# A network in one launch: the norms' sums of squares behind a stage's first tile, their broadcast behind the second

## The chip, the cores and the metric

The kernel runs on one core of one Trainium2 chip. The metric is the time of one execution in microseconds of device time; medians of several runs are compared. The profile is of one further execution, and its times count from the first instruction of that execution to the last (the span).

## The reference

Two models follow one another on a sequence of 256 tokens of width 1024, in fp32. The first has a Mamba-2 mixer, a convolutional feed-forward block, a differential attention and a second feed-forward block; the second has a block with a sparse attention and a recurrent unit, whose normalised input is scaled and shifted by a conditioning vector, then a feed-forward block and a last norm. Each of these parts begins with the same step:

```
def rms_norm(x, g):
    xf = x.astype(jnp.float32)
    y = xf * lax.rsqrt(jnp.mean(xf * xf, axis=-1, keepdims=True) + EPS)
    return y.astype(x.dtype) * g

zxbcdt = rms_norm(x, ln_g) @ in_w                                # mamba
u = causal_dwconv(rms_norm(x, ln_g) @ up_w, conv_w, conv_b)      # ffn
kv = rms_norm(x, kv_ln_g) @ kv_w                                 # attn
xn = rms_norm_2(h, g_mix[l]) * (1.0 + sc1) + sh1                 # dsa
return rms_norm_2(h, g_final)
```

So a norm over the 1024 features of a token stands in front of every large product, and it needs all of x.

## The kernel before

The activations lie with the features on the partitions: x is 8 tiles (k = 0 to 7) of 128 features x 256 tokens. Every weight is streamed from memory (tile raw, by the queue of SP) and split into a high half wh (ScalarE, L253) and a low half wl (VectorE, L257, or in certain places GpSimd, L255, chosen by the table POOLED). The operand x is split alike, into xh and xl. An output tile of 128 rows is 8 k with three matmuls each, xh with wh, xl with wh and xh with wl (L379 to L381), 24 matmuls that accumulate in a PSUM tile mm.

A stage (mamba, ffn0, attn, ffn1, dsa, ffn2, final, in this order) starts as follows. As the stage before ends, add_x makes x tile by tile (L509 or L511), square has ScalarE square each (L440) and GpSimd add the squares of k = 1 to 6 to those of k = 0 in sqacc (L444); the square of k = 7 stays apart. mkraw makes for each k the raw operand rw, g times x without the norm, its high half on ScalarE (L396) and its low half on VectorE (L397). The first four tiles of a stage (NRAW; in mamba one narrow tile of 32 rows, for dt, stands ahead of them) are raw tiles: tileR multiplies the weights with rw, and its postponed part f multiplies the result with the norm afterwards (ru, L412, VectorE, reading PSUM). In dsa and ffn2 f also adds a column, rc (ScalarE, L415). In attn the tokens are the rows of the output, so the norm is a scale of rows and no broadcast is needed.

The norm itself is in rstd_bc: the sums over features are matmuls of squares with ones (L452), sqacc first and the last square behind it, each for two halves of the tokens. rsqrt works out the reciprocal root on VectorE (L296) and GpSimd (L297, to the power of -1/2). Then bcast (L463) spreads it over the partitions by two matmuls with the identity, and ScalarE copies it out as rsb (L484). From rsb VectorE makes for each k the normalised ny (L493), ScalarE xh (L468 or L497) and VectorE xl (L469 or L498), which the tiles from the fifth on read. In mamba and the ffn stages (the table DEFER, which holds how many k go with a step) all this, sums included, is issued at once after the first raw tile (self.pre in tileR); in dsa and attn the sums are issued ahead of the first tile.

What is written in this order isn't what runs: a scheduler puts every engine's instructions in an order of its own, by dependencies and by its costs; after(a, b) tells it that a comes behind b on the same engine. later(n, fn) postpones fn by n tiles. There are three mm tiles in PSUM, and five slots each for wh and wl.

## Time and profile before

| | us |
|---|---|
| median of 3 runs | 1180.02 |
| lowest and highest run | 1178.07, 1181.65 |
| the profiled execution | 1182.38 |
| its span | 1180.6 |

In the profiled execution TensorE is busy for 1124.2 us, VectorE for 961.2, ScalarE for 712.3 and GpSimd for 221.3; the mean granted clock of TensorE is 0.977 of full speed. The page gives the busy time of each engine and the costliest groups; a table lists what TensorE waited for; the timelines give each instruction with its start and length, and in brackets the idle time ahead of it and what ended that. A matmul's length there includes its way through the array, and matmuls overlap, so the cost of one in a row of them is the distance between starts. Each fp32 sum or broadcast matmul of the program shows as two in the trace.

### The profile page before, as it was taken

The numbers are of one execution on the slowest core, as the hardware profiler recorded it, in microseconds if no ns is written. First come the engines' busy times: TensorE is split into PE (matmuls) and PEld (weight loads), VectorE is DVE, ScalarE is ACT, GpSimd is POOL, SyncE is SP. The second block draws the span as 40 slices with busy tenths as digits, with TensorE's granted clock in tenths as the row PEclk, the third lists the DMA queues.
The fourth block names the chain that finished last, engine by engine and source line by source line (L and its number), as shares of the span: only waits on it lengthen the run. The fifth ranks groups of instructions, "written<-read, shape, count | busy, mean of one in ns | idle before, by whom it ended". The sixth has DMA issues, their size and how long they took to land.

```text
span 1180.6 us, 23536 instructions
## 1 busy us (share of the span) xinstructions
PE 1124.2 (95%) x9174; PEld 1093.4 (93%) x9174; DVE 961.2 (81%) x1866; ACT 712.3 (60%) x1322; POOL 221.3 (19%) x180
## 2 busy tenths in 40 slices
PE   6899898999999999999899999899999998999997
PEld 5799887989999999988899999899999998999997
DVE  5887998789898878787899998768967888888752
ACT  6567655566666546877466664465587656666541
POOL 3202665242100114222320001100100023200010
PEclk8899989999999999999799999999999999999999
DMA  8455442647756886663456668754452653554530
GB/s 304 140 179 193 152 161 72 219 166 252 266 201 223 275 288 221 190 224 131 168 198 206 207 215 286 250 194 149 170 170 88 223 197 124 205 189 175 172 137 36
DMA packets 50190, 224.80 MB, mean 190 GB/s; under 512 B 5744, under 2 KB 10496, under 8 KB 31136
## 3 DMA queue, kind: packets, MB, share of 16 engines
q1 hardware_dynamic: 41616, 211.53, 52.1%
q10 hardware_dynamic: 7056, 7.46, 2.1%
q0 software_dynamic: 1408, 4.32, 1.2%
q8 instruction: 72, 1.18, 0.4%
q14 instruction: 38, 0.31, 0.1%
HBM read 222.11 MB, written 4.25 MB: 192 GB/s over the span
## 4 chain that ended last, share of the span: by engine, by line
PE 51%; DVE 17%; issue 7%; DMA 7%; ACT 4%; POOL 1%; ACTq 0%; POOLq 0%; DVEq 0%
PE mm L379 15%; PE mm L380 14%; PE mm L381 14%; DMA ada<-in_wada_dram 7%; DVE wl L257 4%; DVE ada L553 2%; DVE cv L818 2%; ACT wh L253 1%; DVE ny L493 1%; PE mm L790 1%; DVE M L705 1%; PE mm L791 1%; PE mm L789 1%; PE mm L921 1%; PE mm L922 1%
## 5 line engine op out<-in xcount | busy, mean ns | idle before, releaser
L253 ACT ACTIVATE wh<-raw 128x1024 fp32r<-128x1024 f32 (+2 forms) x360 | 369.7, 1030 | 264.9 <-PE mm L380 230.4
L257 DVE TENSOR_TENSOR wl<-raw,wh 128x1024 fp32r<-128x1024 f32 (+1 forms) x333 | 397.9, 1195 | 99.5 <-ACT wh L253 96.7
L379 PE MATMUL mm<-xh,wh 128*128 128x256 f32 x1624 | 465.3, 287 | 8.8 <-DVE cv L818 3.4
L380 PE MATMUL mm<-xl,wh 128*128 128x256 f32 x1624 | 460.6, 284 | 6.3 <-DVE xl L469 6.3
L381 PE MATMUL mm<-xh,wl 128*128 128x256 f32 x1624 | 459.8, 283 | 0.0
L379 PEld LDWEIGHTS mm<-xh,wh 128*128 128x128 f32 x1624 | 308.0, 190 | 15.8 <-issue 6.8
L380 PEld LDWEIGHTS mm<-xl,wh 128*128 128x128 f32 x1624 | 308.0, 190 | 8.2 <-DVE xl L469 7.8
L381 PEld LDWEIGHTS mm<-xh,wl 128*128 128x128 f32 x1624 | 308.0, 190 | 0.3 <-DVE xc L1219 0.3
L444 POOL TENSOR_TENSOR sqacc<-sqacc,sq 128x256 f32<-128x256 f32 x42 | 49.6, 1180 | 558.9 <-ACT sq L440 557.3
L379 PE MATMUL mm<-hh,wh 128*128 128x256 f32 x528 | 147.7, 280 | 0.0
L380 PE MATMUL mm<-hl,wh 128*128 128x256 f32 x528 | 147.5, 279 | 0.0
L381 PE MATMUL mm<-hh,wl 128*128 128x256 f32 x528 | 147.2, 279 | 0.0
L818 DVE SCALAR_TENSOR_TENSOR cv<-mm,par,cv 128x255 f32<-128x255 f32 x240 | 114.2, 477 | 4.4 <-ACT cv L816 2.8
L380 PEld LDWEIGHTS mm<-hl,wh 128*128 128x128 f32 x528 | 99.2, 188 | 0.0
L381 PEld LDWEIGHTS mm<-hh,wl 128*128 128x128 f32 x528 | 99.2, 188 | 0.0
L379 PEld LDWEIGHTS mm<-hh,wh 128*128 128x128 f32 x528 | 99.2, 188 | 0.0
L255 POOL TENSOR_TENSOR wl<-raw,wh 128x1024 fp32r<-128x1024 f32 x27 | 71.9, 2662 | 131.5 <-ACT wh L253 126.3
L553 DVE SCALAR_TENSOR_TENSOR ada<-ada,silu_c 128x512 f32<-128x512 f32 x96 | 71.2, 744 | 20.9 <-DMA ada<-in_wada_dram 20.9
L816 ACT ACTIVATE cv<-mm,par 128x256 f32<-128x256 f32 x120 | 65.6, 547 | 0.0
L379 PE MATMUL mm<-rw,wh 128*128 128x256 f32 (+2 forms) x168 | 51.5, 308 | 10.0 <-ACT wh L253 8.9
L380 PE MATMUL mm<-rw,wh 128*128 128x256 f32 (+2 forms) x168 | 52.5, 312 | 0.0
L381 PE MATMUL mm<-rw,wl 128*128 128x256 f32 (+2 forms) x168 | 51.5, 306 | 0.0
(305 smaller groups left out, 1925.4 us busy)
## 6 DMA issues: line engine op xcount, KB each, us to landing
raw<-in_w_dram SPq DMA_DIRECT2D x148, 1024.0 KB, 4.9
ada<-in_wada_dram SPq DMA_DIRECT2D x96, 256.0 KB, 3.7
raw<-in_w_dram SPq DMA_DIRECT2D x23, 896.0 KB, 4.6
raw<-in_w_dram SPq DMA_DIRECT2D x6, 768.0 KB, 4.4
abc<-acs_scr ACTq DMA_DIRECT2D x16, 256.0 KB, 3.3
rel_bias_scr<-rel_bias_row POOLq DMA_DIRECT2D x8, 384.0 KB, 7.0
bias<-rel_bias_scr ACTq DMA_DIRECT2D x16, 128.0 KB, 2.7
x<-in_xT_dram SPq DMA_DIRECT2D x4, 256.0 KB, 4.5
```

Of the source, the lines that this page charges most:

```text
L253: nc.scalar.activation(wh[:, :n], src, AF.Copy)
L255: nc.gpsimd.tensor_tensor(wl[:, :n], src, wh[:, :n].bitcast(F32), op=ALU.subtract)
L257: self.pace = nc.vector.tensor_tensor(wl[:, :n], src, wh[:, :n].bitcast(F32), op=ALU.subtract)
L379: nc.tensor.matmul(out, h, xh[:, k, :], start=first and a == 0, stop=False)
L380: nc.tensor.matmul(out, h, xl[:, k, :], start=False, stop=False)
L381: nc.tensor.matmul(out, l, xh[:, k, :], start=False, stop=last and a == n - 1)
L444: nc.gpsimd.tensor_tensor(self.acc, self.acc, s, op=ALU.add)
L493: nc.vector.scalar_tensor_tensor(y, self.x[:, k, :], g(k), self.rsb, op0=ALU.mult, op1=ALU.mult)
L553: i = nc.vector.scalar_tensor_tensor(t, t, 1.0, self.sc[:, h * 512:h * 512 + 512], op0=ALU.mult, op1=ALU.mult, accum_out=self.part[:, h, m ...
L705: nc.vector.tensor_tensor(mv[:, h, 0:3:2], e[:, h, 0:3:2, :], CB[:, t // 4, 0:3:2, :], op=ALU.mult)
L816: nc.scalar.activation(c, pt, AF.Identity, scale=w(2), bias=P(cb, ct))
L818: nc.vector.scalar_tensor_tensor(c[:, d:], pt[:, :T - d], w(2 - d), c[:, d:], op0=ALU.mult, op1=ALU.add)
```

## The change

mmB keeps its last matmul. What norm leaves for tileR is now a list of two parts: the sums, which are put behind the last matmul of the first raw tile (by after), and the start (broadcast, rsb and all that follows), put behind the last matmul of the second. The multiplication by the norm of the first raw tile is postponed by one tile more. The square of k = 6 stays apart too, so GpSimd adds those of k = 1 to 5 only, and TensorE sums sqacc and two squares, with six matmul instructions instead of four. dsa gets the same treatment as the ffn stages (DEFER), and in attn the sums stand behind the first half tile (tok). In mamba the load of the silu table, and with it what was flushed there, moves into post_dt.

```diff
-DEFER = {"mamba": 2, "ffn": 8}
+DEFER = {"mamba": 2, "ffn": 8, "dsa": 8}
...
-            nc.tensor.matmul(out, l, xh[:, k, :], start=False, stop=last and a == n - 1)
+            self.last_mm = nc.tensor.matmul(out, l, xh[:, k, :], start=False, stop=last and a == n - 1)
...
+        lag = 1
         if self.pre:
-            self.pre()
-            self.pre = None
+            self.pre.pop(0)(self.last_mm)
+            lag = 2 if len(self.pre) else 1
...
-        self.later(1, f)
+        self.later(lag, f)
...
-        if k == 7:
+        if k == 6:
+            self.sq6 = s
+        elif k == 7:
             self.sq7 = s
...
-    def bcast(self, rs):
+    def bcast(self, rs, behind=None):
...
+            if behind is not None:
+                self.after(mm, behind)
...
-        def start():
-            bc = self.rstd_bc([self.acc, self.sq7], D)
+        def sums(behind=None):
+            self.rstd_bc([self.acc, self.sq6, self.sq7], D, bcast=False, behind=behind)
+
+        def start(behind=None):
+            bc = self.bcast(self.rs, behind)
...
         if self.part_of in DEFER:
-            self.pre = start
+            self.pre = [sums, start]
         else:
+            sums()
             start()
...
+            self.table("silu_and_others")
 
         self.tileR("ssm_in_w", rw, False, post_dt, m=32)
-        self.flush()
-        self.table("silu_and_others")
...
-        self.rstd_bc([self.acc, self.sq7], D, bcast=False)
-        rs = self.rs
...
+                if not norm:
+                    self.rstd_bc([self.acc, self.sq6, self.sq7], D, bcast=False, behind=mm)
+                    norm.append(self.rs)
...
-        self.rstd_bc([self.acc, self.sq7], D, bcast=False)
+        self.rstd_bc([self.acc, self.sq6, self.sq7], D, bcast=False)
```

TensorE at the start of mamba, before: the last matmul of the narrow dt tile (32 rows), the sums (ax from onec and a square), four matmuls of the next raw tile, and the broadcast (ax from con and rs).

```order
L381 MATMUL mm<-rw,wl 32x256
L452 MATMUL ax<-onec,sqacc 128x1 x2
L452 MATMUL ax<-onec,sq 128x1 x2
L379 MATMUL mm<-rw,wh 128x256
L380 MATMUL mm<-rw,wh 128x256
L381 MATMUL mm<-rw,wl 128x256
L379 MATMUL mm<-rw,wh 128x256
L463 MATMUL ax<-con,rs 128x128 x2
```

The same place now, the sums first (the lines of the changed kernel are numbered one to a dozen higher):

```order
L382 MATMUL mm<-rw,wl 32x256
L457 MATMUL ax<-onec,sqacc 128x1 x2
L457 MATMUL ax<-onec,sq 128x1 x4
L380 MATMUL mm<-rw,wh 128x256
L381 MATMUL mm<-rw,wh 128x256
```

And TensorE 24 matmuls further on, where that raw tile ends:

```order
L382 MATMUL mm<-rw,wl 128x256
L470 MATMUL ax<-con,rs 128x128 x2
L380 MATMUL mm<-rw,wh 128x256
L381 MATMUL mm<-rw,wh 128x256
L382 MATMUL mm<-rw,wl 128x256
```

The sums kept their place, with two instructions more, and the broadcast moved from 4 to 24 matmuls behind them.

TensorE at the start of dsa, before, where the sums of sqacc stand ahead of the first raw tile and those of the last square behind 16 of its matmuls:

```order
L452 MATMUL ax<-onec,sq 128x1 x2
L380 MATMUL mm<-rw,wh 128x258
L381 MATMUL mm<-rw,wl 128x258
L379 MATMUL mm<-rw,wh 128x258
L380 MATMUL mm<-rw,wh 128x258
L381 MATMUL mm<-rw,wl 128x258
L379 MATMUL mm<-rw,wh 128x258 x2
L380 MATMUL mm<-rw,wh 128x258
L381 MATMUL mm<-rw,wl 128x258
L463 MATMUL ax<-con,rs 128x128 x2
```

The same place now:

```order
L380 MATMUL mm<-rw,wh 128x258 x2
L381 MATMUL mm<-rw,wh 128x258
L382 MATMUL mm<-rw,wl 128x258
L457 MATMUL ax<-onec,sqacc 128x1 x2
L457 MATMUL ax<-onec,sq 128x1 x4
L381 MATMUL mm<-rw,wh 128x258
```

All sums moved behind the last matmul of the first raw tile (the one in front that counts two has the first matmul of the second tile in it). The broadcast, not in this piece, now stands behind the second raw tile, 48 matmuls ahead of the first one on the normalised x, which was 71 before; in mamba these are 72 and 92, in ffn0 and ffn2 48 and 68, in ffn1 48 and 56.

ScalarE at the start of mamba, before, from the last squares to the copy of the broadcast, rsb:

```order
L440 ACTIVATE sq<-x 128x256 x4
L253 ACTIVATE wh<-raw 128x1024 x2
L484 ACTIVATE rsb<-ax 128x256
L253 ACTIVATE wh<-raw 128x1024
L582 ACTIVATE dtT<-ru 32x256
```

And now:

```order
L443 ACTIVATE sq<-x 128x256 x4
L254 ACTIVATE wh<-raw 128x1024 x4
L496 ACTIVATE rsb<-ax 128x256
L595 ACTIVATE dtT<-ru 32x256
L637 ACTIVATE cv<-ru,par 128x256
```

Two more weight copies stand ahead of rsb. On GpSimd, two of its weight splits in mamba stood on either side of the store of acsT, and now stand ahead of it.

## Rows read from the trace of the kernel before

**Rows 1.** The page's part 1: engine, busy us, share of the span, instructions.
```profile
PE 1124.2 (95%) x9174; PEld 1093.4 (93%) x9174; DVE 961.2 (81%) x1866; ACT 712.3 (60%) x1322; POOL 221.3 (19%) x180
```

**Rows 2.** TensorE's waits: us in total, times, longest us.
```profile
PE ax L452 <- ACT sq L440: 6.4, 2, 4.0
PE ax L463 <- POOL rs L297: 6.3, 5, 3.5
PE mm L380 <- DVE xl L469: 6.3, 5, 2.2
```

**Rows 3.** Windows: stretch, us, busy us (instructions) of each engine, TensorE's granted clock, DMA.
```profile
17.30:24.10 6.80, 5.85 (x27) 5.85 (x28) 3.80 (x6) 3.19 (x6) 2.22 (x2) 0.50 0.78 283
24.10:31.00 6.90, 6.90 (x60) 6.72 (x58) 4.85 (x15) 5.17 (x10) 1.05 (x1) 1.00 0.51 178
563.40:570.20 6.80, 6.80 (x34) 6.80 (x33) 4.59 (x10) 2.65 (x5) 3.46 (x2) 0.50 0.76 262
764.80:771.60 6.80, 6.08 (x28) 6.08 (x29) 3.93 (x10) 2.32 (x5) 1.90 (x3) 0.50 0.79 232
```

**Rows 4.** Timeline, mamba's start: start us, us, engine, line, operation [idle before].
```profile
14.73 1.99 ACT L253 ACTIVATE wh<-raw 128x1024 fp32r<-128x1024 f32 x2
...
15.23 0.61 PE L452 MATMUL ax<-onec,sqacc 128*128 128x1 f32 x4 [1.07 <-POOL sqacc L444]
...
18.25 1.22 PE L463 MATMUL ax<-con,rs 128*128 128x128 f32 x4 [1.39 <-POOL rs L297]
```

**Rows 5.** Timeline, mamba from the dt matmul to the first cv waited for.
```profile
25.51 0.23 DVE L587 TENSOR_TENSOR dtu<-ax,par 128x64 f32<-128x64 f32 x1 [3.25 <-PE ax L585]
...
33.27 6.79 POOL L255 TENSOR_TENSOR wl<-raw,wh 128x1024 fp32r<-128x1024 f32 x2
...
35.35 5.00 DVE L469 TENSOR_TENSOR xl<-ny,xh 128x256 fp32r<-128x256 f32 x2
...
42.92 0.41 DVE L469 TENSOR_TENSOR xl<-ny,xh 128x256 fp32r<-128x256 f32 x1
...
50.84 0.36 PE L379 MATMUL mm<-xh,wh 128*128 128x256 f32 x1 [1.70 <-DVE cv L627]
```

**Rows 6.** Timeline, attn's start: the sums of the last square, the last raw operand.
```profile
435.43 0.60 PE L452 MATMUL ax<-onec,sq 128*128 128x1 f32 x4 [2.45 <-ACT sq L440]
...
436.12 0.48 DVE L397 SCALAR_TENSOR_TENSOR rw<-x,par,rw 128x256 fp32r<-128x256 f32 x1
```

**Rows 7.** Timeline, dsa's start: the same, and the matmul behind the sums.
```profile
765.52 1.02 PE L452 MATMUL ax<-onec,sq 128*128 128x1 f32 x4 [3.98 <-ACT sq L440]
...
766.06 0.48 DVE L397 SCALAR_TENSOR_TENSOR rw<-x,gmdsa,rw 128x256 fp32r<-128x256 f32 x1
...
766.39 0.56 PE L380 MATMUL mm<-rw,wh 128*128 128x258 f32 x1
```

**Rows 8.** Timeline, ffn1's start: the sums, the last raw operand, a late xl.
```profile
561.49 0.61 PE L452 MATMUL ax<-onec,sqacc 128*128 128x1 f32 x4 [0.55 <-POOL sqacc L444]
...
563.78 0.47 DVE L397 SCALAR_TENSOR_TENSOR rw<-x,par,rw 128x256 fp32r<-128x256 f32 x1
...
581.86 0.58 PE L380 MATMUL mm<-xl,wh 128*128 128x256 f32 x1 [2.02 <-DVE xl L469]
```

**Rows 9.** Timeline, ffn0 (three rows) and ffn2 (the last).
```profile
239.72 0.71 PE L463 MATMUL ax<-con,rs 128*128 128x128 f32 x4 [0.45 <-POOL rs L297]
...
240.88 0.42 DVE L412 TENSOR_TENSOR ru<-mm,rsb 128x256 f32<-128x256 f32 x1 [2.00 <-ACT rsb L484]
...
252.25 0.39 PE L380 MATMUL mm<-xl,wh 128*128 128x256 f32 x1 [0.31 <-DVE xl L469]
...
990.25 0.39 PE L379 MATMUL mm<-xh,wh 128*128 128x256 f32 x1 [1.92 <-ACT rc L415]
```

**Rows 10.** Timeline, the last norm's sums.
```profile
1172.56 0.50 PE L452 MATMUL ax<-onec,sqacc 128*128 128x1 f32 x4
1172.92 0.58 PE L452 MATMUL ax<-onec,sq 128*128 128x1 f32 x4
```

## What the change is expected to do

> **What bounds the kernel now.** I read the page first: TensorE is busy 95% of the span [rows 1]. So time is to be had from what TensorE still waits for, and any instruction added to TensorE costs its length unless it falls into such a wait. The table of TensorE's waits comes next [rows 2]: 6.4 us for squares on ScalarE, 6.3 us for the reciprocal root on GpSimd and 6.3 us for the low halves (xl) that VectorE makes. The first two are what the change touches; one 3.5 us piece of the second stands in mamba's inner norm, which is not touched, so some 2.8 us of it is in play. Then the timeline at each of the seven stage starts [rows 4 to 10], and the windows in which TensorE ran at half its clock [rows 3]: 27 instructions filled 5.85 us at 0.50, 60 filled 6.90 us at 1.00. A matmul thus costs 0.217 us at 1.2 GHz and 0.115 us at 2.4 GHz.
>
> **Prices.** One 128x1 sum shows as two passes. Four passes begin at 1172.56 and the next four at 1172.92 [rows 10], so a pass costs 0.09 us at full clock; at half clock four took 0.87, 0.22 each [rows 7]. Each stage has 12 passes instead of 8: 4 more, 0.36 us at full clock. GpSimd loses one add of sqacc a stage.
>
> **The change, stage by stage** (minus is faster). What decides is not the wait that a row names, but whether a second wait stands right behind it.
>
> *mamba.* The sums keep their place behind the narrow dt tile; the broadcast goes from 4 to 24 matmuls behind them. Sums to broadcast took 18.25 - 15.23 = 3.0 us [rows 4]; twelve passes and 24 matmuls are 1.1 + 24 x 0.115 = 3.9 us, so the root is there in time and the wait of 1.39 us goes: -1.4. Passes: +0.4. The 1.07 us in front of the sums [rows 4] ended with the last add on GpSimd, which now isn't needed; the last square, on ScalarE, then ends the wait some 0.4 earlier: -0.4. If the clock no longer falls at 17.3, 27 x (0.217 - 0.115) = 2.7 us come back [rows 3]: -2.7. That is -4.1 by TensorE. VectorE must follow: it sat 3.25 us for the transposed dt matmul at 25.51 [rows 5]. In the new order that matmul stands 26, not 31, behind the broadcast, at about 22, so VectorE's chain starts some 3 us earlier. Behind it the chain is full to the wait for cv at 50.84 (1.70) [rows 5], so the gain is carried only as far as VectorE carries it. ScalarE has four weight copies instead of two ahead of rsb; two took 1.99 from 14.73 [rows 4], so four end near 18.7, about when the broadcast does, and I cost them at nothing (each us that they end later delays the whole chain by one). GpSimd does its second weight split ahead of the store of acsT instead of behind it; the blocked xl pair, 5.00 us against 0.41 for one [rows 5], may move but I see no reason for it to go. I take -4.0; ends -6.2 (4.1 and one blocked xl of 2.1 not met again) and -1.0 (only the wait less the passes).
>
> *attn.* TensorE waited 2.45 us for the last square at 435.43 [rows 6]. But the tile around it needs, for its last k, the low half of the raw operand, which VectorE ends at 436.12 + 0.48 = 436.60, after the square. Without the sums TensorE stops at that instead. The 12 passes now stand behind the tile with nothing to cover them; before, both groups of four lay inside the wait. +1.0 (12 x 0.09). Ends +0.4 and +2.6 (12 x 0.22).
>
> *dsa.* The same: 3.98 us for the square at 765.52, but the low half ends at 766.06 + 0.48 = 766.54, and the sums took until 766.39 [rows 7]. The sums again come uncovered, +1.0 to +2.6; against it stands a stretch from 764.8 at half clock with gaps [rows 3], part of which has tile 2 to fill it. +0.8; ends -2.0 and +3.1 (0.8 and the whole shift below).
>
> *ffn1.* Here the sums waited 0.55 us for GpSimd's add [rows 8]: -0.5, as that add goes and the rest moves up. The low half ends at 564.25 [rows 8], the sums come behind it at half clock: 12 x 0.22 less the 8 that were there, +0.9. The broadcast stands 48 instead of 56 matmuls ahead of the first matmul on the normalised x, so only 8 matmuls less to prepare them; the stretch from 563.4 at half clock [rows 3] and the 2.02 us for a blocked xl at 581.86 [rows 8] may each shrink; I take 0.4 and 1.0. -1.0; ends -2.6 and +1.5.
>
> *ffn0, ffn2.* Raw operands are ready, so the wait for the root goes: 0.45 at 239.72 [rows 9], about the same in ffn2, paid back by 0.36 of passes. But the broadcast comes 20 matmuls, 20 x 0.115 = 2.3 us, later, and the first matmul on the normalised x 48 instead of 68 behind it. VectorE, which idled 2.00 us for rsb [rows 9], idles some 1.9 more, and one low half came 0.31 late already [rows 9]. The new order of TensorE puts raw matmuls between those on the first normalised k, which covers most of the shift: ffn0 +0.5, ends -1.5 and +2.3. In ffn2 the wait of 1.92 for rc [rows 9] sits in ScalarE's order behind the same chain; it may go or be replaced: 0, ends -1.9 and +2.3.
>
> *final.* The sums stand on the closing chain: 4 passes, +0.4. The square had long been there, so the lost add gives nothing.
>
> GpSimd issues ffn0's bias rows earlier and SP swaps two loads in ffn1; nothing on TensorE waits for either there, so they cost nothing while these loads are ahead.
>
> **Sum:** -4.0 + 1.0 + 0.8 - 1.0 + 0.5 + 0 + 0.4 = -2.3 us. The profiled execution took 1182.38 us (span 1180.6), 2.4 above the median of 1180.02; -2.3 puts such an execution at 1180.1 and the median at **1177.7 us**.
>
> **Rivals.** (A) *The normalised x becomes late; slower.* The place is VectorE behind rsb, 2.3 us later in ffn0, dsa and ffn2. If all of it shows: ffn0 +2.3, dsa +3.1, ffn2 +2.3, mamba only -2.5, with attn +1.0, ffn1 0 and final +0.4: +6.6, 1186.6 us. It decides once the new waits in these three exceed 2.3 us together. For it speaks that a low half was late in ffn0 already; against it the raw matmuls now placed in between, and that dsa ran without a wait after its broadcast. VectorE's two-operand instructions are blocked while GpSimd splits a weight: 5.00 us for two, beside GpSimd's 6.79 [rows 5]. The Trainium skill states this as a rule (SBUF — State Buffer, "Who interferes with whom"): a DVE instruction with two SBUF inputs and a GpSimd instruction that reads SBUF hold off each other for a whole instruction. The trace agrees; by that rule one more such meeting in mamba would make its term -1.9 and the sum -0.2.
>
> (B) *Everything goes as meant; clearly faster.* No half clock in mamba (-6.2), and in ffn1 and dsa the stretches at 0.50 shrink too. Each held about 30 instructions, 30 x 0.1 = 3 us, so ffn1 -2.6 and dsa -2.0, the rest as above: -6.2 + 1.0 - 2.0 - 2.6 + 0.5 + 0 + 0.4 = -8.9, 1171.1 us. For it: the clock fell behind waits [rows 3, 4]. Against it: in attn, dsa and ffn1 the waits stay. The Trainium skill (TensorE: Matmul & The Clock Gate, "Part 1: The HAM clock gate") says that the throttled clock is the default and that activity releases it. By that rule a gap merely moved in dsa and attn throttles as before, which is against (B) there, while in mamba 2.7 us would come back; the 0.50 rows agree.
>
> (C) *It does nothing.* In mamba the gain stops at VectorE (-1.0); the others as forecast: +0.7, 1180.7 us.
>
> **How the numbers follow.** Forecast 0.45 (its own range 1174.5 to 1181), A 0.20, B 0.20, C 0.15. About 0.3% of the time, 3.5 us, is what a measurement of this kernel can tell from no change. Faster by more: B whole and somewhat under half of the forecast, 0.40. Slower by more: most of A, and a little of C, 0.17. Within: 0.43. The range leaves out the outer half of A and of B: 1171.5 to 1184.5.
>
> **What would show it.** Right, if in the changed profile the broadcast waits for nothing in mamba, ffn0 and ffn2; if in attn and dsa TensorE's wait is still 2 to 4 us but ends on the low half, with twelve passes behind; if the granted clock from 17 to 24 us is 1.00 and the last xl of mamba ends near 41, the tile after it by 47. Wrong, if low halves or cv are waited for at the first normalised k of ffn0, dsa or ffn2 (A), or if mamba's wait at 50.84 comes at the same time as before (C).

## The result, and the profile after

The changed kernel takes 1194.14 us, the median of six runs (1184.37 to 1196.26); the kernel before, beside it, 1180.63 (1178.07 to 1182.81). The ratio, worked out from all runs and not from the two medians, is 1.0102, with a 95% interval of 1.0078 to 1.0127. That is slower by 9 to 15 us, beyond the upper end of the range (1184.5), where 2.3 us faster was forecast. The profiled execution took 1196.26 us, with a span of 1194.5 and a mean granted clock of 0.973.

The page's part 1 of the changed kernel (engine, busy us, share, instructions; [rows 1] before):

```profile
PE 1132.8 (95%) x9202; PEld 1102.0 (92%) x9202; DVE 956.7 (80%) x1866; ACT 712.1 (60%) x1322; POOL 216.9 (18%) x173
```

TensorE idles 61.7 us of the span where it idled 56.4, and is busy 8.6 us more. VectorE, ScalarE and GpSimd work as long as before or less. So of the 13.9 us by which the two spans differ, 5.3 are waiting. The 8.6 are in the main the 28 passes more (2.5 us at the 0.09 of [rows 10]) and time at half clock: the span times (1 - mean granted clock) went from 27.0 to 32.6 us. TensorE's waits in the changed kernel (us in total, times, longest), beside [rows 2]:

```profile
PE mm L380 <- ACT hh L477: 4.8, 1, 4.8
PE ax L470 <- POOL rs L298: 4.5, 3, 3.5
PE mm L931 <- ACT rw L397: 4.4, 1, 4.4
...
PE mm L381 <- DVE xl L478: 3.0, 5, 1.5
PE mm L380 <- DVE cv L639: 2.8, 1, 2.8
...
PE mm L381 <- DVE xl L510: 2.3, 1, 2.3
```

The change did what it says: the 6.4 us for squares are gone, and the broadcast waits for nothing in mamba, ffn0 and ffn2 (what is left under rs is 3.5 in mamba's inner norm, which isn't touched, and two pieces of 0.5). In their place stand waits that the table of before doesn't have: hh 4.8, rw 4.4, xl of L510 2.3; and the one for cv in mamba grew from 1.7 to 2.8.

To place the loss I cut each stage at two matmuls of TensorE that lie outside the changed order, the same two in every profile, and compared the time between them: in the two profiles, and as means over profiles in which the stage is changed in full (2 to 5 of them) and in which it is as before (10 to 15), those of the experiments below among them.

| stretch | forecast (ends) | profile before, after | mean as before, changed | difference of means |
|---|---|---|---|---|
| mamba's start | -4.0 (-6.2 to -1.0) | 135.2, 135.3 | 134.9, 132.6 | -2.3 |
| ffn0 | +0.5 (-1.5 to 2.3) | 63.3, 69.6 | 63.3, 69.6 | **+6.3** |
| attn | +1.0 (0.4 to 2.6) | 28.8, 33.5 | 30.6, 32.4 | +1.8 |
| ffn1 | -1.0 (-2.6 to 1.5) | 57.3, 57.5 | 56.5, 57.4 | +0.9 |
| dsa | +0.8 (-2.0 to 3.1) | 84.7, 85.2 | 83.1, 87.1 | **+4.0** |
| ffn2 | 0 (-1.9 to 2.3) | 37.0, 38.7 | 36.8, 38.2 | +1.4 |
| ffn2's end | no term | 146.7, 147.0 | 146.7, 147.0 | +0.3 |
| the last norm | +0.4 | 23.3, 23.7 | 23.3, 23.7 | +0.4 |

The differences of the means add up to +12.8; the medians differ by 13.5, the means of the six runs each by 11.8. The profile of before stands 1.8 below the mean of its kind in attn and 1.6 above it in dsa, so a comparison of just two profiles would have put 4.7 us on attn and 0.5 on dsa. How far one stretch varies between profiles: dsa 78.9 to 85.2 as before and 85.2 to 88.9 changed; attn 28.6 to 33.0 and 31.5 to 33.5, so that attn's difference is not clear of the scatter; mamba 133.6 to 135.6 and 131.0 to 135.3; ffn0 63.3 and 69.6 in every one.

**ffn0.** Timelines of the changed kernel (start us, us, engine, line, operation, and in brackets the idle time ahead), GpSimd first, then VectorE, ScalarE and TensorE:

```profile
255.12 0.60 POOL L870 DMA_DIRECT2D rel_bias_row<-rev  x1 [7.09 <-ACT rev L869]
257.18 0.74 POOL L873 DMA_DIRECT2D rel_bias_scr<-rel_bias_row  x1 [1.46 <-DMA rel_bias_row<-rev]
257.94 2.42 POOL L256 TENSOR_TENSOR wl<-raw,wh 128x1024 fp32r<-128x1024 f32 x1
260.28 2.08 POOL L873 DMA_DIRECT2D rel_bias_scr<-rel_bias_row  x3
262.47 2.71 POOL L256 TENSOR_TENSOR wl<-raw,wh 128x1024 fp32r<-128x1024 f32 x1
...
257.38 4.07 DVE L258 TENSOR_TENSOR wl<-raw,wh 128x1024 fp32r<-128x1024 f32 x1
...
262.90 2.55 DVE L830 SCALAR_TENSOR_TENSOR cv<-ru,par,cv 128x254 f32<-128x254 f32 x1
...
266.21 0.42 ACT L477 ACTIVATE hh<-cv 128x256 fp32r<-128x256 f32 x1 [3.83 <-DVE cv L840]
...
266.72 0.55 PE L380 MATMUL mm<-xh,wh 128*128 128x256 f32 x1 [4.83 <-ACT hh L477]
```

And GpSimd at the same work in the kernel before:

```profile
260.90 3.44 POOL L255 TENSOR_TENSOR wl<-raw,wh 128x1024 fp32r<-128x1024 f32 x1 [5.78 <-ACT wh L253]
267.96 2.48 POOL L255 TENSOR_TENSOR wl<-raw,wh 128x1024 fp32r<-128x1024 f32 x1 [3.62 <-ACT wh L253]
273.55 0.60 POOL L858 DMA_DIRECT2D rel_bias_row<-rev  x1 [3.11 <-DVE cv L818]
```

To be read from bottom to top: TensorE stands 4.83 us for hh, which ScalarE makes of a cv that VectorE brings late, because two of VectorE's instructions took 4.07 and 2.55 us. Both overlap a GpSimd split. With no GpSimd split beside it, a VectorE split took 1.21 us (at 266.88 in the same timeline) and a cv 0.47. The first of the two GpSimd splits had its high half at 253.14 (ScalarE, 252.10 + 1.04) and began at 257.94: ahead of it in GpSimd's queue stood the store of a bias row, which waited for ScalarE's rev, and a copy that waited 1.46 us more for that store. Before, the first bias row came only at 273.55, behind the first five splits.

**mamba.** TensorE's sums and broadcast and its two longest waits, then VectorE beside GpSimd, in the changed kernel ([rows 4, 5] before):

```profile
14.00 0.61 PE L457 MATMUL ax<-onec,sqacc 128*128 128x1 f32 x4 [0.41 <-POOL sqacc L449]
...
19.76 0.66 PE L470 MATMUL ax<-con,rs 128*128 128x128 f32 x4
...
31.32 0.43 PE L618 MATMUL ax<-av,con 128*128 128x64 f32 x2 [1.81 <-DVE av L615]
...
47.83 0.55 PE L380 MATMUL mm<-xh,wh 128*128 128x256 f32 x1 [2.78 <-DVE cv L639]
...
27.99 2.61 DVE L505 SCALAR_TENSOR_TENSOR ny<-x,par,rsb 128x256 f32<-128x256 f32 x1
...
26.72 3.60 POOL L256 TENSOR_TENSOR wl<-raw,wh 128x1024 fp32r<-128x1024 f32 x1 [5.37 <-ACT wh L254]
...
34.23 6.20 POOL L256 TENSOR_TENSOR wl<-raw,wh 128x1024 fp32r<-128x1024 f32 x1 [0.30 <-ACT wh L254]
```

Sums to broadcast took 5.8 us without a wait. VectorE's chain follows 1.7 us earlier (dtu at 23.77, 25.51 before), not 3, and then meets GpSimd's splits: one ny takes 2.61 instead of 0.47, and TensorE waits 1.81 for av, which VectorE makes. At 40 us TensorE was 6 us ahead of the kernel before; at 55 us 0.3. What took it back, by windows (us, busy us (instructions) of each engine, granted clock, DMA share and GB/s), first before, then after, then the same 63 matmuls in a kernel whose mamba is changed alike (the first experiment below):

```profile
41.00:55.00 14.00, 12.30 (x86) 12.02 (x86) 12.46 (x28) 7.79 (x16) 0.00 (x0) 0.87 0.45 152
```

```profile
41.20:55.00 13.80, 11.00 (x63) 10.57 (x64) 10.56 (x25) 6.58 (x12) 0.00 (x0) 0.75 0.46 154
```

```profile
39.90:51.05 11.15, 8.35 (x63) 7.99 (x64) 10.56 (x26) 6.63 (x12) 0.00 (x0) 1.00 0.47 156
```

63 matmuls instead of 86 in the stretch: the wait for cv is 1.1 longer, and more of it lies at half clock (0.75 against 0.87). The third window shows which of the two counts for more. That kernel waits alike (1.81 us for av, 2.80 for cv), and VectorE is held by GpSimd's splits alike (2.59 for one ny); but its clock was 1.00, and the 63 matmuls took 11.15 us. Its lead on the kernel before goes from 6.8 us to 4.3 in this stretch, and here from 6.6 to 0.3. In the other two profiles with mamba changed in full, TensorE is 4.3 and 2.3 us ahead at the same place, with a clock of 1.00 and 0.87 over these matmuls. So where the clock stays at 1.00 the stretch takes some 2.5 us of the lead, with its waits behind VectorE; the rest that was lost here goes with half clock.

**attn.** ScalarE's last square and operand, then TensorE, in the changed kernel ([rows 6] before):

```profile
443.90 0.42 ACT L443 ACTIVATE sq<-x 128x256 f32<-128x256 f32 x1 [2.69 <-DVE x L522]
...
444.23 0.49 ACT L397 ACTIVATE rw<-x,par 128x256 fp32r<-128x256 f32 x1
...
444.77 0.58 PE L931 MATMUL mm<-wh,rw 128*128 128x256 f32 x1 [4.38 <-ACT rw L397]
...
445.97 0.85 PE L457 MATMUL ax<-onec,sqacc 128*128 128x1 f32 x4
446.68 1.84 PE L457 MATMUL ax<-onec,sq 128*128 128x1 f32 x8
448.39 0.56 PE L931 MATMUL mm<-wh,rw 128*128 128x256 f32 x1
```

The wait moved from the square to the operand behind it in ScalarE's queue, and the twelve passes now cost 448.39 - 445.97 = 2.42 us, at half clock, with nothing to cover them. In each of the five profiles in which they stand there they took 2.41 or 2.42 us.

**dsa.** TensorE in the changed kernel ([rows 7] before):

```profile
774.46 0.50 PE L380 MATMUL mm<-rw,wh 128*128 128x258 f32 x2 [1.67 <-ACT rw L397]
...
775.48 0.50 PE L457 MATMUL ax<-onec,sqacc 128*128 128x1 f32 x4
775.84 1.03 PE L457 MATMUL ax<-onec,sq 128*128 128x1 f32 x8
776.74 0.37 PE L381 MATMUL mm<-rw,wh 128*128 128x258 f32 x1
...
814.19 0.92 PE L891 MATMUL ax<-kid,qi 64*128 64x128 f32 x4 [1.27 <-DMA kid<-kw]
```

The same shift of the wait to the operand, and 776.74 - 775.48 = 1.26 us of passes (2.42 at half clock in two of the experiments' profiles). A new place is 814.19, some 40 us behind the change: index keys that a DMA copies from kw to kid, for which TensorE waited 0.26 us before.

**ffn2.** TensorE, and VectorE beside GpSimd, in the changed kernel ([rows 9] before):

```profile
1001.10 0.51 PE L380 MATMUL mm<-xh,wh 128*128 128x256 f32 x2 [0.83 <-ACT xh L509]
...
1006.48 0.58 PE L381 MATMUL mm<-xl,wh 128*128 128x256 f32 x1 [2.34 <-DVE xl L510]
...
1003.27 2.48 POOL L256 TENSOR_TENSOR wl<-raw,wh 128x1024 fp32r<-128x1024 f32 x1 [6.55 <-ACT wh L254]
...
1003.46 2.58 DVE L830 SCALAR_TENSOR_TENSOR cv<-ru,par,cv 128x254 f32<-128x254 f32 x1
```

The wait of 1.92 for rc is gone, and 0.83 + 2.34 took its place (2.33 to 2.35 in all four profiles with ffn2 changed in full). GpSimd's third split holds a cv of VectorE for 2.58 us while two low halves are still to be made. Before, a cv was held the same way (2.62 us at 995.22, beside the split at 994.01), but 15 us behind the broadcast (979.41), where all low halves stood ready; now the meeting comes 10 us behind it (993.10). An earlier one before (2.62 us at 984.67) made no low half late, as TensorE came to the first normalised k only at 990.25.

### The profile page after: what moved, and what is told of

Same layout as the page of the kernel before. It is cut to its first block, busy times and chain, and to the rows that moved or that the text cites. A ratio compares the mean times of both kernels' runs of the same rounds, so it can differ in the third digit from the quotient of the medians.

```text
span 1194.5 us, 23575 instructions
## 1 busy us (share of the span) xinstructions
PE 1132.8 (95%) x9202; PEld 1102.0 (92%) x9202; DVE 956.7 (80%) x1866; ACT 712.1 (60%) x1322; POOL 216.9 (18%) x173
## 4 chain that ended last, share of the span: by engine, by line
PE 55%; DVE 15%; issue 8%; ACT 5%; DMA 5%; POOL 1%; ACTq 0%; POOLq 0%; DVEq 0%
PE mm L380 15%; PE mm L381 15%; PE mm L382 15%; DMA ada<-in_wada_dram 4%; DVE wl L258 4%; DVE cv L830 2%; DVE ada L566 2%; ACT wh L254 1%; PE mm L802 1%; PE mm L801 1%; PE mm L803 1%; ACT L L289 1%; DVE ny L505 1%; PE ax L891 1%; PE mm L931 1%
## 5 line engine op out<-in xcount | busy, mean ns | idle before, releaser
L258 DVE TENSOR_TENSOR wl<-raw,wh 128x1024 fp32r<-128x1024 f32 (+1 forms) x333 | 402.0, 1208 | 105.4 <-ACT wh L254 102.8
L449 POOL TENSOR_TENSOR sqacc<-sqacc,sq 128x256 f32<-128x256 f32 x35 | 42.1, 1203 | 564.0 <-ACT sq L443 563.7
```

The source lines that it names most:

```text
L258: self.pace = nc.vector.tensor_tensor(wl[:, :n], src, wh[:, :n].bitcast(F32), op=ALU.subtract)
L449: nc.gpsimd.tensor_tensor(self.acc, self.acc, s, op=ALU.add)
```

## The experiments

The changed kernel was given two sets of stages: PRE, those whose sums and broadcast stand behind the first and the second tile, and SQ6, those with the third square. Full, they give the changed kernel, and empty, the kernel before. Ratios are to the kernel before, timed beside each on the same chip, over all runs; before's medians lay between 1180.5 and 1182.5. The us given for a stretch are those of the one profile of a run.

**First question: GpSimd's order in ffn0, or the normalised x that comes later (rival A)?** The changed kernel with ffn0's bias rows held behind the splits that were issued ahead of them, as before:

```diff
-            nc.gpsimd.tensor_tensor(wl[:, :n], src, wh[:, :n].bitcast(F32), op=ALU.subtract)
+            self.pwl = nc.gpsimd.tensor_tensor(wl[:, :n], src, wh[:, :n].bitcast(F32), op=ALU.subtract)
...
-            nc.gpsimd.dma_start(row, r)
+            self.after(nc.gpsimd.dma_start(row, r), self.pwl)
```

(and the same for the copies of L873).

> The changed kernel with one order restored: in ffn0 the store and the copies of the bias rows on GpSimd's queue stand behind its weight splits again (row behind the fourth, copies behind the sixth); every other engine's order is that of the changed kernel. Theory Q (GpSimd's queue: the rows' wait for a DMA holds the splits back, and the splits then block VectorE): the 4.83 us wait in ffn0 at 266.72 goes, about 6 us less, 1188. Rival N (VectorE is late in ffn0 because rsb is late, the rows are innocent): still 1194. Rival D (the rest of the loss hangs on where the loads stand in time): with ffn0 earlier, attn's wait of 4.38 changes too, 1183 to 1188.

Measured: 1191.32 us, ratio 1.0074 (1.0047 to 1.0102). In ffn0 the 4.83 us wait is gone, and the stretch took 64.0 us, 0.7 above the mean as before. But the median came down by 3 us only, and the two intervals overlap. So the order is what ffn0 loses by, and not the whole loss. ffn0 alone, and all but ffn0:

```diff
+PRE = {"ffn0"}
+SQ6 = {"ffn0"}
```

> The kernel before, with the change made in ffn0 alone (sums behind the first raw tile, broadcast behind the second, third square on TensorE there). GpSimd's order in ffn0 is then that of the changed kernel. Q and N: the loss of ffn0 alone, +6, 1186.5. D: the later stages wait longer as well although their code is untouched, attn up to +5: 1191.

Measured: 1186.47, 1.0047 (1.0030 to 1.0063), and 69.6 us in the stretch, with the same wait for hh, 4.89 us.

```diff
+PRE = {"mamba", "attn", "ffn1", "dsa", "ffn2"}
+SQ6 = {"mamba", "attn", "ffn1", "dsa", "ffn2", "final"}
```

> The changed kernel with ffn0 as before. Q and N: 1194 - 6 = 1188, attn's wait of 4.4 us on the raw operand stays since attn is changed. D: attn's wait is not its own, it falls to about the 2.5 us of before plus the passes: 1183 to 1184.

Measured: 1196.39 in four runs, 1.0123 (1.0087 to 1.0160). It wasn't faster than the changed kernel, although ffn0 in its profile is as before; that profile (1190.23) is the fastest of the four runs, and what the other three lost isn't seen (their mean granted clock was 0.971 to 0.973, that of the profile 0.977). The intervals of both overlap, so this run only says that the other stages together lose several us too. ffn0 alone with GpSimd's order restored (both edits):

```diff
+PRE = {"ffn0"}
+SQ6 = {"ffn0"}
...
-            nc.gpsimd.dma_start(row, r)
+            self.after(nc.gpsimd.dma_start(row, r), self.pwl)
```

> As e2 (the kernel before with the change in ffn0 alone), with GpSimd's order restored as in e1. Theory Q: e2 lost 5.2 us inside ffn0 in its trace and 5.9 us in its median (1186.5); with the order restored about 1 us stays: 1181.5, and the wait of more than 4 us behind ScalarE's hh is not there. Rival N (the late rsb costs it): 1186 again. What e1's median told was unclear, since the runs of that kernel scatter over 12 us.

Measured: 1183.78, 1.0015 (0.9993 to 1.0038), and 64.0 us in the stretch. GpSimd there, the splits ahead of the bias row again:

```profile
252.20 2.54 POOL L261 TENSOR_TENSOR wl<-raw,wh 128x1024 fp32r<-128x1024 f32 x1 [5.20 <-ACT wh L259]
263.19 3.37 POOL L261 TENSOR_TENSOR wl<-raw,wh 128x1024 fp32r<-128x1024 f32 x1 [8.46 <-ACT wh L259]
266.52 0.60 POOL L891 DMA_DIRECT2D rel_bias_row<-rev  x1
```

The split at 252.20 came 7.6 us behind the one ahead of it; in the changed kernel that distance is 12.3. Two edits that differ in GpSimd's order alone give 69.6 and 64.0 us in ffn0: that is shown. In all they give 1.0047 and 1.0015, whose intervals overlap a little. What is left of ffn0 (0.7) is near the term of the forecast; TensorE there waits 1.55 us for a low half, which is rival A at less than its price.

**Second question: the other stages, one at a time.**

```diff
+PRE = {"mamba"}
+SQ6 = {"mamba"}
```

> The kernel before with the change in mamba alone. By the trace of the changed kernel mamba's start gains 0.3 us by 55 us and the half clock from 175 to 210 costs 2.6: 1180 to 1183. If that half clock is chance and not the change: 1180.3. The forecast's term was -4.0: 1176.6.

Measured: 1179.01, 0.9993 (0.9963 to 1.0023), with runs from 1174.21 to 1188.69. The interval holds the 2.3 us that mamba's stretch gains in the mean, and no gain.

```diff
+PRE = {"attn"}
+SQ6 = {"attn"}
```

> The kernel before with the change in attn alone. Forecast's term +1.0 (twelve passes behind the wait for the low half, uncovered): 1181.6. Rival D (attn's loss is the phase of the loads for the conditioning vector, which the shift from the stages ahead set): then nothing ahead is shifted here, and attn loses only the passes, 1181 to 1182; the traces of e1, after and e3 showed +2.3 to +4.8 there. If attn's own order is the cause: 1183 to 1185.

Measured: 1183.99, 1.0033 (1.0019 to 1.0048).

```diff
+PRE = {"dsa"}
+SQ6 = {"dsa"}
```

> The kernel before with the change in dsa alone. The traces of the changed kernel, e1 and e3 show +0.5, +1.6 and +4.2 in dsa, of which some 2 where TensorE waits for the copy of kw to kid (1.3 to 1.9 us, 0.3 before). If dsa's own order makes this: 1182 to 1183. If it came with the shift of the stages ahead: 1181.4, the forecast's +0.8.

Measured: 1186.52, 1.0056 (1.0036 to 1.0076).

```diff
+PRE = {"ffn2"}
+SQ6 = {"ffn2"}
```

> The kernel before with the change in ffn2 alone. Rival A of the prediction (VectorE's normalised x comes late behind the later rsb): +1.0 to +2.1 as in the three traces with it, 1182 to 1182.7, with waits for xh and xl at the first normalised k. The forecast's term was 0: 1180.6.

Measured: 1185.87, 1.0044 (1.0028 to 1.0060). So attn, dsa and ffn2 each lose by themselves. Their ratios come to 3.9, 6.6 and 5.2 us, where the stretches show 1.8, 4.0 and 1.4; with ffn0's 5.5, and mamba's -0.8, they add up to 20, and the changed kernel loses 12. The parts don't add up; why a stage alone loses more in all than in its own stretch wasn't found. Part of it is time at half clock: by the span times (1 - clock) the runs of these three lost 27.3, 29.2 and 27.2 us in the mean, and the kernel before beside them 25.0.

**Third question: which part of the change loses there?** My theory by then was that the later broadcast costs. All sums moved, and the broadcast issued at once behind them:

```diff
-            sums()
+            sums(behind if self.stage in PRE else None)
             start()
...
-        if self.stage in PRE:
-            self.pre = [sums, start]
-        elif defer:
+        if defer:
             self.pre = [both]
```

> The changed kernel in all stages, but the broadcast and all behind it issued right behind the sums, as before (a few matmuls behind them instead of behind the second raw tile). Sums behind the first tile with three squares, dsa deferred, attn as changed. GpSimd's order in ffn0 is then again that of before. Theory B (the loss is what follows from the later broadcast: GpSimd's order in ffn0, VectorE late in dsa and ffn2): only the uncovered passes stay, about +1.0 each in attn and dsa, 0.4 in the others: 1183 to 1184. Rival S (the loss is the sums and their passes behind the wait): 1190 or more.

Measured: 1193.59, 1.0097 (1.0064 to 1.0129): as slow, but not in the same places. In its profile GpSimd's splits stand ahead of the bias rows again, as before, and ffn0 took 64.7 us (69.6 in the changed kernel); ffn2 took 40.9 (38.7), at a granted clock of 0.87 (0.96). All moved, but two squares as before (eight passes):

```diff
-SQ6 = {"mamba", "ffn0", "attn", "ffn1", "dsa", "ffn2", "final"}
+SQ6 = set()
```

> The changed kernel with the sums and broadcasts moved, but GpSimd adding the square of k = 6 as before and TensorE summing two parts (8 passes, not 12, in seven places). B: seven times 0.36 less, 1191 to 1192. S: more than that, since in attn and dsa the passes fall into half clock, 1188 to 1189; but the sums in ffn1 wait for GpSimd's last add again (+0.5).

Measured: 1192.62, 1.0091 (1.0055 to 1.0127). And the third square alone, in all stages, with the old order:

```diff
-PRE = {"mamba", "ffn0", "attn", "ffn1", "dsa", "ffn2"}
+PRE = set()
```

> The kernel before with only the third square: GpSimd adds one less, TensorE sums three parts, sums and broadcasts stand where they stood. 7 x 0.36 = 2.5 us of passes at full clock; in attn and dsa two of the three parts lie inside the wait for the last square, and ffn1's and mamba's waits for the add (0.55 and 0.4) go: about +1, 1181.6. S would put it at 1184 or more.

Measured: 1183.59, 1.0021 (0.9995 to 1.0046). So the third square isn't what makes most of the loss, and the moved sums, with it, are enough for a loss of the same size. As the cause of the whole, the later broadcast fell; in ffn0 it does cost, since GpSimd's order changes with it. It fell in dsa by itself too, where only the sums, with their third square, were moved:

```diff
+PRE = {"dsa"}
+SQ6 = {"dsa"}
...
-            sums()
+            sums(behind if self.stage in PRE else None)
             start()
...
-        if self.stage in PRE:
-            self.pre = [sums, start]
-        elif defer:
+        if defer:
             self.pre = [both]
```

> The kernel before with dsa alone changed, and there only the sums moved behind the first raw tile (three squares); the broadcast follows right behind them as before. e7, with both, lost 6.0 us in its mean. Theory S (the sums' twelve passes, uncovered and at half clock, and the gap ahead of them in one piece): most of it is here, 1184 to 1187. Theory B (the later broadcast): 1181 to 1182.

Measured: 1185.44, 1.0026 (1.0011 to 1.0041), and 87.6 us in dsa's stretch. And only the broadcast:

```diff
+PRE = {"dsa"}
+SQ6 = set()
...
-            self.pre = [sums, start]
+            sums()
+            self.pre = [lambda behind: None, start]
```

> The complement: in dsa the sums stay (sqacc ahead of the first tile, the last square inside it, two squares), and the broadcast and what follows stand behind the second raw tile. B: 1184 to 1187. S: 1180.5 to 1182.

Measured: 1181.71, 1.0004 (0.9986 to 1.0021), and 82.5 us, where the mean as before is 83.1. The two intervals overlap; the stretches are further apart. In attn, which has no broadcast, the third square alone:

```diff
+PRE = set()
+SQ6 = {"attn"}
```

> The kernel before with attn's third square on TensorE alone, the sums where they stood. e6 (moved and three squares) lost 3.4 us in its mean. The sums of sqacc and of k = 6 stand ahead of the tile and in the wait, so: 0 to +0.4, 1180.6 to 1181.

Measured: 1180.33, 0.9995 (0.9982 to 1.0009). And the sums moved with two squares:

```diff
+PRE = {"attn"}
+SQ6 = set()
```

> The kernel before with attn's sums moved behind the first half tile, two squares (8 passes). If the passes behind the wait cost what they cost at half clock, two thirds of e6's 12: 8 x 0.22 = 1.8, 1182.4. If the forecast's full clock holds: +0.7, 1181.3. If the place costs more than its passes (the gap ahead in one piece lowers the clock for longer): 1183 to 1184.

Measured: 1183.35, 1.0012 (0.9994 to 1.0030). Neither half of attn's change can be told from nothing; both together lose 1.0033. Of attn's stretch 2.42 us is what the uncovered passes take; the eight of before took 0.83 to 1.34.

dsa's loss can be cut finer, over the seven profiles in which its sums are moved and the twelve in which they and the broadcast are not: by the means 1.7 us are lost in the first two hundred matmuls, around the raw tiles and the sums, and 2.0 in the fifty around kid. In the two hundred TensorE waits no longer than before (2.9 and 3.0 us), so what is lost there is the uncovered passes and time at half clock. Of the 2.0 us around kid, 0.8 is a longer wait for kid, and 1.2 the matmuls behind it, which took longer (the granted clock was 0.86 from 810 to 822 us in the changed kernel, and 1.00 from 800 to 812 before). TensorE waited for kid 1.27, 1.85, 1.82, 0.53, 2.36, 0.56 and 0.85 us in the seven, 1.3 in the mean, and 0.5 in the mean of the twelve (0.18 to 0.67, and one of 1.93); with the broadcast alone moved it was 0.78, and the 1.93 is that of the third square alone. The stretch from the issue of that load to its landing, before and after (windows, columns as above):

```profile
801.10:804.00 2.90, 2.68 (x18) 1.98 (x17) 1.47 (x3) 1.80 (x3) 0.54 (x1) 1.00 0.69 285
```

```profile
810.20:814.20 4.00, 2.73 (x20) 2.05 (x18) 2.56 (x6) 1.80 (x3) 0.57 (x1) 1.00 0.51 201
```

TensorE has 2.7 us of work to cover the load in both. The load took 2.9 us and then 4.0 (up to 5.0 in the run with all sums moved), while the DMA engines were less busy, 0.51 against 0.69. So in these two it isn't more traffic that delays it. The longer wait goes with the moved sums in the mean, with an overlap; by what way isn't settled.

**Fourth question: is VectorE beside GpSimd's splits the limit, as in ffn0, also where the change gained?** In mamba, the changed stage with GpSimd's splits of tiles 3 and 5 given back to VectorE:

```diff
+PRE = {"mamba"}
+SQ6 = {"mamba"}
...
-POOLED = {"ffn": (1, 3, 5, 7, 9, 11), "mamba": (1, 3, 5, *range(22, 44, 4))}
+POOLED = {"ffn": (1, 3, 5, 7, 9, 11), "mamba": (1, *range(22, 44, 4))}
```

> As e4 (the change in mamba alone), and two of the weight splits at mamba's start done by VectorE instead of GpSimd (POOLED loses 3 and 5). In the trace of the changed kernel VectorE's ny was blocked for 2.61 and 2.26 us beside GpSimd's splits there, 0.47 each without; two splits on VectorE cost 1.2 us each. If these meetings are where mamba's gain stops: about 1.5 us less than e4, 1178.5, and better than the kernel before. If VectorE is simply full: no gain, 1180 to 1181.

Measured: 1178.27, 0.9966 (0.9942 to 0.9989). That beats the kernel before, but the interval overlaps that of mamba alone, and mamba's stretch took 132.0 us, near its mean of 132.6. The same in the kernel before, with nothing of the change:

```diff
-POOLED = {"ffn": (1, 3, 5, 7, 9, 11), "mamba": (1, 3, 5, *range(22, 44, 4))}
+POOLED = {"ffn": (1, 3, 5, 7, 9, 11), "mamba": (1, *range(22, 44, 4))}
```

> The control: the kernel before with the same two splits on VectorE. There a pair of xl was blocked (5.00 us for two against 0.41 each) by GpSimd's pair of splits, so some 2 to 4 us less on the way to the tile at 50.84 against 2.4 us more work on VectorE: 1179 to 1181. If e16 gains and this doesn't, the gain belongs to the change.

Measured: 1177.06, 0.9958 (0.9939 to 0.9976). It gains as much without the change, so the gain belongs to the splits; mamba's stretch took 129.8 us, where the mean as before is 134.9. The window to be compared with those of mamba above:

```profile
41.00:55.00 14.00, 12.39 (x99) 11.98 (x99) 13.38 (x26) 9.67 (x20) 0.00 (x0) 1.00 0.58 190
```

99 matmuls where the kernel before has 86 and the changed one 63, at a granted clock of 1.00, with VectorE busy 13.38 us of 14 (12.46 and 10.56). The long VectorE rows of [rows 5] have no counterpart. Last, in the kernel before, the same with tiles 3 and 5 of each feed-forward stage given back as well:

```diff
-POOLED = {"ffn": (1, 3, 5, 7, 9, 11), "mamba": (1, 3, 5, *range(22, 44, 4))}
+POOLED = {"ffn": (1, 7, 9, 11), "mamba": (1, *range(22, 44, 4))}
```

> The kernel before, with the late GpSimd splits of the mamba stage done by VectorE (as in the run before this one) and, new, the feed-forward stages' splits with GpSimd as helper cut from six tiles of twelve to four (1, 7, 9, 11). If a GpSimd split beside VectorE's chain holds VectorE up in the feed-forward stages as it did in mamba (blocked operations of 2.3 to 2.6 us there), this gains a further 1 to 3 us over the 1177.1 of the run with mamba's splits alone: 1174 to 1176. If VectorE has no room in these stages, its own longer work takes it back: 1177 or above. If neither, 1177.1 within its interval.

Measured: 1174.56, 0.9942 (0.9919 to 0.9965), the fastest of all. The further step isn't separated from the one before it, whose interval overlaps; in the profile ffn0's stretch took 61.8 us against 63.3.

## Why the prediction was wrong

The forecast was 2.3 us faster, and the change is some 12 us slower. By its steps:

- **The step that failed first** is the last sentence on the change: "GpSimd issues ffn0's bias rows earlier ...; nothing on TensorE waits for either there, so they cost nothing while these loads are ahead." It looked for a direct wait on the bias rows. The price lay in what is queued behind them on GpSimd: the third split came 4.7 us later and met VectorE's chain at the point where it feeds TensorE. It cost 5.6 us in ffn0's stretch (+6.3 against a term of +0.5), from two profiles that differ in that order alone. The condition of the sentence, that the loads are ahead, covers the rows and not the splits behind them. Such a meeting is what the rule cited in rival A is about (the Trainium skill, SBUF — State Buffer, "Who interferes with whom"); here a VectorE split took 4.07 us beside a GpSimd one, instead of 1.21. I applied it to mamba and not to ffn0.
- **dsa** (+0.8 forecast, +4.0 in the stretch, above its end of 3.1). The shift of the wait to the operand and the uncovered passes came as written, 1.26 us for the passes in this profile and 2.42 in two others, against 1.1 taken and 2.6 as the upper end. The term left out everything behind the first tiles; half of the loss lies around kid, 0.8 us of it a longer wait and the rest slower matmuls, and of this the forecast has no row.
- **attn** (+1.0, +1.8, within its ends). The mechanism was right, except that the high half from ScalarE ended the wait, not the low half. The size was off because the passes ran at half clock, 2.42 us, the price that the forecast had as its upper end (2.6); before, too, the sums behind such waits ran at half clock [rows 7], so it should have been the value taken.
- **ffn2** (0, +1.4) and **ffn1** (-1.0, +0.9): within their ends, both on the wrong side. In ffn2 rc's wait was replaced, as feared, by a late low half, the mechanism of rival A, at 2.34 us. In ffn1 the broadcast still waited 0.49 us at 579.44.
- **mamba** (-4.0, -2.3, within its ends). The broadcast waits for nothing, and ScalarE's four copies ended at 18.2, ahead of it, as written. Of the tests set, this profile fails: the clock from 17 to 24 was 0.80 and not 1.00, the last low half ended at 42.6 and not 41, the tile at 47.83 began behind 2.78 us for cv. The three other profiles with mamba changed in full pass: the clock there was 1.00, VectorE's chain (dtu) began 3.1 us earlier, the last low half ended at 41.2 to 41.6, and the tile after it began at 46.5 to 46.9, though behind 2.80 us for cv. Two of them keep 4.3 us at 55 us, one 2.3, this one 0.3. So the mechanism was right; what the forecast put into its sum whole, that the clock no longer falls, held in some executions and not in others. It isn't rival C: the waits behind VectorE are the same where 4.3 us stay.
- **final** (+0.4, +0.4): right. The +0.3 at ffn2's end has no term.

Rival A, 1186.6 us, came nearest, and its mechanism was seen in ffn2 and, smaller, in ffn0. But what it names, the later broadcast, isn't what costs in all: with the broadcast back behind the sums the whole time was the same (1.0097), and in dsa alone the stretch took 82.5 us for the broadcast against 87.6 for the sums. In ffn0 the later broadcast does cost, by GpSimd's queue, which rival A doesn't name. The stretches account for 12.8 us. What delays kid, why half clock falls in one execution and not in another, what the single stages lose beyond their own stretches, and why the run with all but ffn0 isn't faster than the changed kernel stay open.

## What to carry to other kernels

A wait that is taken away at one engine is worth what the next wait behind it leaves: look up the next operand in the queue of the producer, here the raw operand right behind the square. A reordering has to be priced on every queue that it disturbs, by what stands *behind* each moved instruction there; a DMA issue that waits holds back the instructions behind it on its engine (here a split whose operand was there at 253.14 began at 257.94). A gain seen or missed in one profile can be the clock of that execution: look at the same matmuls in several profiles before naming a wait as the cause. And a helper engine is worth its help only where its instructions don't meet the chain that it helps: VectorE's own split takes 1.2 us, GpSimd's 2.4 and more, with up to 2 to 3 us of VectorE's time lost beside it.

## What the runs showed of the hardware

- Executions of one kernel scatter with the mean granted clock. The changed kernel's six runs go from 1184.37 us at 0.982 to 1196.26 at 0.973, mamba alone from 1174.21 at 0.985 to 1188.69 at 0.972. Between the kernels the clock tells less: span times (1 - clock) is 26.0 us in the mean over 130 runs of the kernel before and 28.8 over the six of the changed one, 2.8 of the 11 us by which the means differ. The run with all sums moved and the broadcast behind them lost 33.4 that way, so two kernels alike in time were slow in different ways.
- One and the same order of work kept a gain or lost it with the clock: with mamba changed in full, TensorE was 4.3, 4.3, 2.3 and 0.3 us ahead at 55 us in four profiles, with a granted clock from 17 to 24 us of 1.00, 1.00, 1.00 and 0.80 and, over the same 63 matmuls around 41 to 55 us, of 1.00, 1.00, 0.87 and 0.75, and with the same wait for cv (2.8 us).
- The same DMA copy of 64 KB (kid) took 2.9 to 5.0 us from issue to landing, and was slower in two profiles in which the DMA engines were less busy (0.51 and 0.54 against 0.69).
- Splits taken from GpSimd and given back to VectorE, which is 81% busy [rows 1] against GpSimd's 19%, made the kernel faster: by 0.42% (0.24 to 0.61) with two of mamba's and by 0.58% (0.35 to 0.81) with two of each feed-forward stage as well. Both beat the kernel before and the changed one.
